# Half-array matmuls that take turns, in a decoder trunk on one core

## The chip, the core and the metric

The kernel runs on one core of a Trainium2 chip. TensorE multiplies: a stationary tile of up to 128 x 128 is loaded (a weight load, PEld in the profile), then a second operand streams through it. A product whose stationary tile has 64 columns or 64 rows uses half of the array. VectorE (DVE), ScalarE (ACT) and GpSimd (POOL) do the rest, SyncE (SP) issues the DMAs. The metric is the device time of one execution in microseconds, lower is better.

## What is computed

Two layers of a trunk over 1024 tokens of width 1024, all in f32. Each layer projects its input, runs three token mixers side by side, projects back, and ends with a gated convolutional feed-forward part. The parts of the reference that matter:

```python
# stick-breaking attention, 4 heads of 64, per block of 128 queries
z = einsum('bhqd,bhkd->bhqk', qb, k) * scale
log_keep = where(past, log_sigmoid(-z), 0.0)
log_later = cumsum(log_keep, axis=3, reverse=True) - log_keep
w = where(past, exp(log_sigmoid(z) + log_later), 0.0)
out = einsum('bhqk,bhkd->bhqd', w, v)

# softmax attention (MLA), 4 heads, queries and keys of 96, values of 64
p = softmax(where(causal, q @ k.T * scale, neg))
out = einsum('bhqk,bhkd->bhqd', p, v)

# RWKV-7, 8 heads of 64: a recurrence over tokens
sa = state @ -kk_t
state = state * w_t + outer(sa, kk_t * a_t) + outer(v_t, k_t)
y_t = state @ r_t
```

## The kernel before

Each layer goes through the same stages. First the projections with the first part of RWKV woven in (`phase_a`): `rw_stage1` handles two heads of 64 channels stacked on 128 partitions, in chunks of 64 tokens, and multiplies keys by queries within each chunk (L662). Head 0 lies in partitions 0 to 63, head 1 in 64 to 127, so each product has 64 rows: 4 products for head 0 into one PSUM bank, then 4 for head 1 into another. `rw_chain` then carries the state from chunk to chunk; its matmuls (L839, L847) write 64 partitions each, with 64 columns streaming. L839 goes to the two column halves in turns, L847 does one half of a chunk pair after the other.

Then attention. Four generators yield one block of 128 queries at a time: two softmax heads (`mla`, hp 0 and 1) and two stick-breaking heads (`stick`, hp 0 and 1). Each generator first goes through a head of pair 0 with key length growing from 128 to 1024, then through one of pair 1 with it shrinking from 1024 to 128; at the change of pair it loads and splits the new queries and keys. For stick-breaking pair 1 that split (L361, in four pieces each for q and k) is on GpSimd. `run` sorts the blocks of the four generators by step plus an offset, `STREAM_ORDER`, given in the order softmax 0, stick 0, softmax 1, stick 1.

A block makes its scores on TensorE (L202 to L204 with the mask product L539 for softmax, L376 and L377 for stick-breaking), weights on ScalarE, VectorE and GpSimd (L384 is the causal mask of stick-breaking, L385 to L388 the scan and product), transposes the weights 128 columns at a time (L327), copies them to one of six buffers `wt4` (L328) and multiplies by the values (`attn_out`, L312):

```python
for j in range(nb):
    self.nc.tensor.matmul(av, V[:, j, :], wt[:, j, :], start=j == 0, stop=j == nb - 1)
```

`V[:, j, :]` has 128 columns: the values of both heads of the pair. The result has 128 partitions, of which `av_store` copies the 64 of this head (L399) and stores them to DRAM. An f32 matmul appears as two records in the profile.

After attention, `oproj` multiplies the mixers' outputs by `w_o`, first split into high and low parts (`woh`, `wol`, `w0h`, `w0l`), and the feed-forward part follows.

What sets the order: every engine runs its instructions in a fixed order. A scheduler makes it when the kernel is built; it takes the program's order, the `PRIORITY` offsets of the helpers, and which buffers are free. A pool's buffers come free when the last reader is done.

Of the kernel before, what the change touches and what calls it, by code (L numbers as in the profile page):

```python
# [17 lines left out]
P = 128  # L18
# [12 lines left out]
C = 64  # L31
# [8 lines left out]
SPLIT_MLA = (0, 0)  # L40
SPLIT_STICK = (0, 4)
MLA_AHEAD = 4
STREAM_ORDER = (-3, 0, 0, 1)
Y_LAG = 2
PRIORITY = {
    "wload": 100,
# [23 lines left out]
class Body:  # L70
    def __init__(self, ctx, tc, a):
        self.ctx, self.tc, self.nc, self.a = ctx, tc, tc.nc, a
        self.n = 0
        self.ptags = {}
        self.rot = 0
        self.sq = 0
        self.sn = self.kn = 0

    def nm(self, s):
        self.n += 1  # L80
        return f"{s}_{self.n}"
# [20 lines left out]
    def ps1(self):  # L102
        return self.pst("ps")
# [203 lines left out]
            nc.vector.scalar_tensor_tensor(d[:, o + 1 : o + 512], ps[:, :511], mu, d[:, o + 1 : o + 512], op0=ALU.mult, op1=ALU.add)  # L307
        return d

    def attn_out(self, wt, nb, V, av):  # L310
        for j in range(nb):
            self.nc.tensor.matmul(av, V[:, j, :], wt[:, j, :], start=j == 0, stop=j == nb - 1)  # L312

    def pieces(self, LL):
        if LL <= 512:
# [65 lines left out]
    def stick_post(self, be, kp, i, LL, nb, n, V, hp, pr, wp):  # L381
        nc = self.nc
        dg = be[:, i * P : LL]
        nc.gpsimd.affine_select(out=dg, in_=dg, pattern=[[-1, P]], base=0, channel_multiplier=1, compare_op=ALU.is_gt, fill=-1.0)  # L384
        nc.vector.tensor_scalar(kp[:, : LL - 1], be[:, 1:LL], -0.5, 0.5, op0=ALU.mult, op1=ALU.add)  # L385
        kv = kp[:, : LL - 1][:, ::-1]
        nc.vector.tensor_tensor_scan(kv, kv, self.ones.to_broadcast([P, LL - 1]), 1.0, op0=ALU.mult, op1=ALU.mult)
        nc.vector.scalar_tensor_tensor(be[:, :LL], be[:, :LL], 1.0, kp[:, :LL], op0=ALU.add, op1=ALU.mult)  # L388
        wt = self.w_transpose(self.wt4[:, n % 6], be, nb, "pa")
        self.av_store(wt, nb, V, hp, self.mixd[pr], i, wp, "pa", 0.5)  # L390

    @prioritized
    def av_store(self, wt, nb, V, hp, dst, i, wp, tag, sc=1.0):
        nc = self.nc
        hr = slice(hp * 64, hp * 64 + 64)
        av = self.pst(tag)[:, :P]
        self.attn_out(wt, nb, V, av)
        ot = self.t(wp, [P, P], "avo", bufs=2)
        nc.scalar.mul(ot[hr], av[hr], sc)  # L399
        nc.sync.dma_start(dst[hr, i * P : i * P + P], ot[hr])  # L400

    def exact2(self, ps, st, src, tp, rows=slice(0, P)):
        hi, lo = (self.t(tp, [P, W2], n, F32R) for n in ("sh", "sl"))
# [145 lines left out]
    def mla_post(self, st, e, pcs, n, nb, sc, pr, hp, i, V, wp):  # L549
        nc = self.nc  # L550
        if n == 1:
            nc.vector.reciprocal(st[:, 6:7], st[:, 4:5])
        else:
            nc.scalar.activation(st[:, 7:8], st[:, 0:1], AF.Exp, scale=sc, bias=st[:, 3:4])
            nc.vector.scalar_tensor_tensor(st[:, 5:6], st[:, 4:5], st[:, 7:8], st[:, 5:6], op0=ALU.mult, op1=ALU.add)
            nc.vector.reciprocal(st[:, 6:7], st[:, 5:6])
        for u, (a0, a1) in enumerate(pcs):
            if u < n - 1:
                nc.vector.tensor_scalar(e[:, a0:a1], e[:, a0:a1], st[:, 7:8], st[:, 6:7], op0=ALU.mult, op1=ALU.mult)
            else:  # L560
                nc.vector.tensor_scalar(e[:, a0:a1], e[:, a0:a1], st[:, 6:7], None, op0=ALU.mult)
        self.sn += 1
        wt = self.w_transpose(self.wt4[:, self.sn % 6], e, nb)
        self.av_store(wt, nb, V, hp, self.mixd[2 + pr], i, wp, "av")

    def q2(self, tp):
        return self.t(tp, [P, W2], "q2", bufs=self.q2n)
# [33 lines left out]
    def rw_stage1(self, ft, hf, rkv, prep, Aa, tp):  # L601
        nc = self.nc
        tk = slice(hf * W2, hf * W2 + W2)
        pr_, pk, pvv = (t[:, tk] for t in rkv)
        L_, av, kk = (t[:, tk] for t in prep)
        ps1 = self.ps2
# [10 lines left out]
        AR = self.q4(tp).rearrange("p (a j e i) -> p a j e i", a=2, e=2, i=C)  # L617
        BK = self.q4(tp).rearrange("p (j e x i) -> p j e x i", e=2, x=2, i=C)
# [20 lines left out]
        flat = lambda t: t.rearrange("p a i -> p (a i)")  # L639
        for g in range(2):  # L640
            js = slice(2 * g, 2 * g + 2)
            RB = self.t(tp, [P, 2, 4, P], "RB", bufs=2)
            X = self.t(tp, [P, 2, 2, P], "X", bufs=2)
            pt = ps1()
            for q in range(2):
                j = 2 * g + q
                nc.tensor.transpose(pt[:, q * P : q * P + P], flat(AR[:, 0, j]), self.ident)
                nc.tensor.matmul(pt[:, (2 + q) * P : (3 + q) * P], pvv[:, j * P : j * P + P], self.cent, start=True, stop=True)
            pa = pt[:, 0:256].rearrange("p (q h k) -> p h q k", q=2, h=2)
            for h in range(2):  # L650
                nc.scalar.copy(X[:, h, :, h * C : h * C + C], pa[:, h])
            nc.scalar.copy(Vt[:, js, :], pt[:, 256:512].rearrange("p (q v) -> p q v", q=2))
            pb = ps1()
            for cc in range(4):
                nc.tensor.transpose(pb[:, cc * P : cc * P + P], flat(BK[:, 2 * g + cc // 2, cc % 2]), self.ident)
            pbv = pb.rearrange("p (c h k) -> p h c k", c=4, h=2)
            nc.scalar.copy(RB[:, :, :, C:P], pbv)
            for h in range(2):
                hr = slice(h * C, h * C + C)
                pA = ps1()  # L660
                for cc in range(4):
                    nc.tensor.matmul(pA[:, cc * P : cc * P + P], flat(BK[hr, 2 * g + cc // 2, cc % 2]), AR[hr, :, 2 * g + cc // 2, cc % 2, :], start=True, stop=True)  # L662
                pAv = pA.rearrange("p (c x) -> p c x", x=P)
                mk = self.maskA
                nc.vector.tensor_tensor(Aa[:, h, HC * hf + 4 * g : HC * hf + 4 * g + 4, :], pAv[:, :, 0:C], mk[:, None, 0:C].to_broadcast([P, 4, C]), op=ALU.mult)
                nc.vector.tensor_tensor(RB[:, h, :, 0:C], pAv[:, :, C:P], mk[:, None, C:P].to_broadcast([P, 4, C]), op=ALU.mult)
            pkv = ps1()[:, :256].rearrange("p (h q v) -> p h q v", h=2, q=2)
            for h in range(2):
                for q in range(2):
                    j = 2 * g + q  # L670
                    for e in range(2):
                        kr = slice(64 - 64 * e, 128 - 64 * e)
                        orow = slice(64 * e, 64 * e + 64)
                        nc.tensor.matmul(pkv[orow, h, q, :], Aa[kr, h, HC * hf + 2 * j + e, :], Vt[kr, j, h * C : h * C + C], start=True, stop=True)
            for h in range(2):
                nc.scalar.copy(X[:, h, :, C - h * C : P - h * C], pkv[:, h])
            gj = slice(4 * hf + 2 * g, 4 * hf + 2 * g + 2)
            RBv = RB.rearrange("p h (j e) x -> p h j (e x)", e=2)
            for h in range(2):
                nc.sync.dma_start(self.rbd[gj, :, 2 * ft + h].rearrange("j p x -> p j x"), RBv[:, h])  # L680
                nc.sync.dma_start(self.xxd[gj, :, 2 * ft + h].rearrange("j p x -> p j x"), X[:, h])
# [435 lines left out]
    def run(self):  # L1117
        nc, a, tc = self.nc, self.a, self.tc
# [27 lines left out]
        for l in range(L):  # L1146
# [7 lines left out]
            with ExitStack() as c:  # L1154
                self.psum(c, mm=(512, 3))
                self.psum(c, pi=(512, 1))
                cc = ExitStack()
# [4 lines left out]
            with ExitStack() as c:  # L1162
                self.psum(c, sc=(512, 2), av=(512, 2))
                aw = self.pool(c, "attn", bufs=2, side=side)
                ms = [self.mla(aw, hp) for hp in range(2)]
                self.wt4 = self.t(self.ip, [P, 6, NT, P], "Aa")
                self.kp3 = [self.t(self.ip, [P, S], n) for n in ("LA", "T", "pd")]
                for t in self.kp3:
                    nc.gpsimd.memset(t, 0.0)
                for _ in range(MLA_AHEAD):  # L1170
                    next(ms[0])
                cc.close()
                self.w0h = self.t(self.wq, [P, 2, D], "w0h", F32R)
                self.w0l = self.t(self.wq, [P, 2, D], "w0l", F32R)
                aw3 = self.pool(c, "attn3", bufs=2, side=other)
                st = [self.stick(aw3, self.ip, hp) for hp in range(2)]
                seq = sorted([(t + o, n, g) for n, (g, o) in enumerate(zip((ms[0], st[0], ms[1], st[1]), STREAM_ORDER)) for t in range(17)], key=lambda x: x[:2])
                for _, _, g in seq:
                    next(g, None)
                nxt = self.mix_load(NT - 1)  # L1180
                wr = [self.wo_load(l, k) for k in range(6)]
                for k in range(2):
                    self.split(self.w0h[:, k], self.w0l[:, k], wr[k], nc.gpsimd)
# [45 lines left out]
```

## Time and profile before

| | |
|---|---|
| runs before | 3151.69, 3152.36, 3153.42 us; median 3152.36 |
| profiled execution | 3154.05 us, span 3152.3 us |
| TensorE busy | 2993.2 us, 95% of the span, granted clock 0.981 on average |
| VectorE busy | 1796.4 us, 57% |
| ScalarE busy | 1058.6 us, 34% |
| GpSimd busy | 330.7 us, 10% |
| layer 0: attention | from 556.9 to about 746 us |
| layer 1: attention | from 2110.4 to about 2305 us |

Busy shares are means over stages with different limits; the rows further down give the stretches apart. A busy TensorE is not one at its peak: its matmuls overlap, and a record's length holds the time that its result needs to drain.

### The profile page before, as it was taken

The numbers are of one execution on the slowest core, as the hardware profiler recorded it, in microseconds if no ns is written. First come the engines' busy times: TensorE is split into PE (matmuls) and PEld (weight loads), VectorE is DVE, ScalarE is ACT, GpSimd is POOL, SyncE is SP. The second block draws the span as 40 slices with busy tenths as digits, with TensorE's granted clock in tenths as the row PEclk, the third lists the DMA queues.
The fourth block names the chain that finished last, engine by engine and source line by source line (L and its number), as shares of the span: only waits on it lengthen the run. The fifth ranks groups of instructions, "written<-read, shape, count | busy, mean of one in ns | idle before, by whom it ended". The sixth has DMA issues, their size and how long they took to land. (4 is left out here: it accounts for less than half of the span.)

```text
span 3152.3 us, 42021 instructions
## 1 busy us (share of the span) xinstructions
PE 2993.2 (95%) x16572; PEld 2421.2 (77%) x16572; DVE 1796.4 (57%) x2842; ACT 1058.6 (34%) x1865; POOL 330.7 (10%) x346
## 2 busy tenths in 40 slices
PE   8998999988999999999999989999789999999998
PEld 6677777776888888888877767777678888888887
DVE  4587764876644444444746877567865444344436
ACT  5444343764122112222144443446532211122220
POOL 0112131132000000000001111311310000000000
PEclk9999899999999999999999999999899999999999
DMA  4344566323421111111234456662235111111111
GB/s 129 97 141 110 169 186 191 97 62 121 149 85 50 51 41 47 54 50 51 64 84 127 108 132 193 178 190 53 81 121 172 54 47 40 43 56 49 54 47 54
DMA packets 339284, 301.79 MB, mean 96 GB/s; under 512 B 25224, under 2 KB 304016, under 8 KB 339088
## 3 DMA queue, kind: packets, MB, share of 16 engines
q1 hardware_dynamic: 339088, 299.11, 32.1%
q8 instruction: 131, 2.15, 0.3%
q14 instruction: 65, 0.53, 0.1%
HBM read 208.87 MB, written 90.18 MB: 95 GB/s over the span
## 5 line engine op out<-in xcount | busy, mean ns | idle before, releaser
L202 PE MATMUL psmm<-xTh,whi 128*128 128x512 f32 x2144 | 852.9, 398 | 0.0
L204 PE MATMUL psmm<-xTh,wlo 128*128 128x512 f32 x2144 | 852.1, 397 | 0.0
L203 PE MATMUL psmm<-xTl,whi 128*128 128x512 f32 x2144 | 852.1, 397 | 0.0
L197 ACT CAST whi<-raw 128x1024 fp32r<-128x1024 f32 x152 | 159.9, 1052 | 1111.3 <-PE psmm L203 1076.1
L204 PEld LDWEIGHTS psmm<-xTh,wlo 128*128 128x128 f32 x2144 | 405.2, 189 | 93.2 <-issue 4.3
L202 PEld LDWEIGHTS psmm<-xTh,whi 128*128 128x128 f32 x2144 | 405.4, 189 | 92.9 <-issue 4.4
L203 PEld LDWEIGHTS psmm<-xTl,whi 128*128 128x128 f32 x2144 | 405.3, 189 | 92.8 <-issue 3.9
L198 DVE TENSOR_TENSOR wlo<-raw,whi 128x1024 fp32r<-128x1024 f32 x122 | 148.8, 1220 | 424.5 <-ACT whi L197 424.5
L1031 DVE TENSOR_TENSOR y<-y,psps 128x512 f32<-128x512 f32 x288 | 196.2, 686 | 171.8 <-PE psps L204 171.4
L202 PE MATMUL psps<-wdh,hh 128*128 128x512 f32 x672 | 266.8, 397 | 0.0
L203 PE MATMUL psps<-wdl,hh 128*128 128x512 f32 x672 | 263.1, 391 | 0.0
L204 PE MATMUL psps<-wdh,hl 128*128 128x512 f32 x672 | 260.1, 391 | 0.0
L894 POOL TENSOR_TENSOR lrs<-lrs,mhalf 128x1 f32<-128x1 f32 x32 | 29.1, 910 | 1637.7 <-DVE lrs L893 1637.7
L202 PEld LDWEIGHTS psps<-wdh,hh 128*128 128x128 f32 x672 | 126.1, 188 | 36.4 <-ACT hh L197 5.5
L204 PEld LDWEIGHTS psps<-wdh,hl 128*128 128x128 f32 x672 | 126.2, 188 | 27.0
L203 PEld LDWEIGHTS psps<-wdl,hh 128*128 128x128 f32 x672 | 126.3, 188 | 25.8
L1006 DVE TENSOR_TENSOR cv<-cv,psmm 128x1024 f32<-128x1024 f32 x44 | 53.7, 1221 | 143.3 <-PE psmm L204 138.4
L198 DVE TENSOR_TENSOR wdl<-raw,wdh 128x1024 fp32r<-128x1024 f32 x42 | 51.4, 1225 | 88.5 <-ACT wdh L197 88.5
L198 POOL TENSOR_TENSOR wlo<-raw,whi 128x1024 fp32r<-128x1024 f32 x30 | 76.0, 2532 | 242.5 <-ACT whi L197 242.4
L312 PE MATMUL pspa<-Aa,mv 128*128 128x128 f32 x576 | 86.4, 298 | 4.4 <-ACT Aa L328 3.8
L312 PEld LDWEIGHTS pspa<-Aa,mv 128*128 128x128 f32 x576 | 77.1, 207 | 17.5 <-ACT Aa L328 15.8
L820 PE MATMUL pspa<-RBl,PSl 128*128 128x128 f32 x512 | 73.4, 292 | 17.2 <-ACT QC L823 11.8
(443 smaller groups left out, 4777.4 us busy)
## 6 DMA issues: line engine op xcount, KB each, us to landing
raw<-in_ffn_w_up_dram SPq DMA_DIRECT2D x88, 512.0 KB
raw<-in_w_in_dram SPq DMA_DIRECT2D x44, 512.0 KB
raw<-in_ffn_w_down_dram SPq DMA_DIRECT2D x44, 512.0 KB
rbd<-RB SPq DMA_DIRECT2D x64, 256.0 KB
PSl<-psd SPq DMA_DIRECT2D x32, 512.0 KB
RBl<-rbd SPq DMA_DIRECT2D x32, 512.0 KB
psd<-Vz SPq DMA_DIRECT2D x64, 128.0 KB
xxd<-X SPq DMA_DIRECT2D x64, 128.0 KB
```

Source lines behind the costliest of these rows:

```text
L197: self.nc.scalar.copy(hi, src)
L198: (eng or self.nc.vector).tensor_tensor(lo, src, hi.bitcast(F32), op=ALU.subtract)
L202: mm(out, lh, rh, start=start, stop=False)
L203: mm(out, lh, rl, start=False, stop=False)
L204: mm(out, ll, rh, start=False, stop=stop)
L312: self.nc.tensor.matmul(av, V[:, j, :], wt[:, j, :], start=j == 0, stop=j == nb - 1)
L820: nc.tensor.matmul(pQ[:, f, e, :], PSh[:, f, h, e, :], RBh[:, f, h, e, :], start=True, stop=True)
L894: nc.gpsimd.tensor_tensor(rs, rs, self.mhalf[:, 0:1], op=ALU.pow)
L1006: nc.vector.tensor_tensor(cv, cv, pg, op=ALU.mult)
L1031: nc.vector.tensor_tensor(y[:, i, hs], y[:, i, hs], ps, op=ALU.add)
```

## The change

Four edits. `attn_out` takes the weights of both heads of a pair and multiplies each by its own 64 value columns, into its own 64 partitions of one PSUM tile, head 0 and head 1 in turns. For that, `pair` holds the first head's weights until the second's are there; then one copy and one store carry both. In `rw_stage1` the 8 key-query products of a group go to the two row halves in turns, with both PSUM banks taken at the start. `in_order` adds dependencies that keep these turns on TensorE. And the generators' offsets become (-2, 0, -2, 0), with the four softmax blocks that run ahead shared by the two heads.

```diff
-STREAM_ORDER = (-3, 0, 0, 1)
+STREAM_ORDER = (-2, 0, -2, 0)
...
+    def in_order(self, ms):
+        for a, b in zip(ms, ms[1:]):
+            self.tc.add_manual_dep(b.ins, a.ins.name, mybir.DependencyInfo(mybir.DependencyClass.NoSync, mybir.DependencyReason.DATA), reason="array halves take turns")
+
-    def attn_out(self, wt, nb, V, av):
+    def attn_out(self, wts, nb, V, av):
+        ms = []
         for j in range(nb):
-            self.nc.tensor.matmul(av, V[:, j, :], wt[:, j, :], start=j == 0, stop=j == nb - 1)
+            for hp in range(2):
+                hc = slice(hp * 64, hp * 64 + 64)
+                ms.append(self.nc.tensor.matmul(av[hc], V[:, j, hc], wts[hp][:, j, :], start=j == 0, stop=j == nb - 1))
+        self.in_order(ms)
...
-        self.av_store(wt, nb, V, hp, self.mixd[pr], i, wp, "pa", 0.5)
+        self.pair(("s", pr, i), wt, hp, nb, V, self.mixd[pr], i, wp, "pa", 0.5)
+
+    def pair(self, key, wt, hp, *args):
+        if key in self.pairs:
+            wts = [wt, wt]
+            wts[1 - hp] = self.pairs.pop(key)
+            self.av_store(wts, *args)
+        else:
+            self.pairs[key] = wt
...
-        nc.scalar.mul(ot[hr], av[hr], sc)
-        nc.sync.dma_start(dst[hr, i * P : i * P + P], ot[hr])
+        nc.scalar.mul(ot, av, sc)
+        nc.sync.dma_start(dst[:, i * P : i * P + P], ot)
...
+            pAs = [ps1(), ps1()]
+            ms = []
+            for cc in range(4):
+                for h in range(2):
+                    hr = slice(h * C, h * C + C)
+                    ms.append(nc.tensor.matmul(pAs[h][:, cc * P : cc * P + P], flat(BK[hr, 2 * g + cc // 2, cc % 2]), AR[hr, :, 2 * g + cc // 2, cc % 2, :], start=True, stop=True))
+            self.in_order(ms)
             for h in range(2):
-                hr = slice(h * C, h * C + C)
-                pA = ps1()
-                for cc in range(4):
-                    nc.tensor.matmul(pA[:, cc * P : cc * P + P], flat(BK[hr, 2 * g + cc // 2, cc % 2]), AR[hr, :, 2 * g + cc // 2, cc % 2, :], start=True, stop=True)
-                pAv = pA.rearrange("p (c x) -> p c x", x=P)
+                pAv = pAs[h].rearrange("p (c x) -> p c x", x=P)
...
-                for _ in range(MLA_AHEAD):
-                    next(ms[0])
+                for t in range(MLA_AHEAD):
+                    next(ms[t % 2])
```

In the changed file the lines are 9 to 19 further down: L320 is the value product (before L312), L336 the transposes (L327), L370 the split on GpSimd (L361), L393 the mask (L384), L385 and L386 the stick-breaking scores (L376, L377). In the rows that follow a size is that of the result, and "x4" counts matmuls that stand unbroken.

TensorE, first half of attention in layer 0. Before, with softmax value products (psav) and stick-breaking ones (pspa) beside transposes of weights (mexp):

```order
L312 MATMUL psav_5400<-Aa_4944,mv_4951 128x128 x2
L312 MATMUL pspa_5433<-Aa_4944,mv_5237 128x128
L327 MATMUL psav_5460<-ident_60,mexp_5439 128x128 x4
L327 MATMUL psav_5466<-ident_60,mexp_5439 128x128 x3
L327 MATMUL pspa_5493<-ident_60,mexp_5482 128x128
L377 MATMUL pspq_5530<-kl_945_5414,qh_943_5412 128x256
L327 MATMUL pspa_5493<-ident_60,mexp_5482 128x128 x2
L202 MATMUL pssc_5552<-kh_920_5311,qh_918_5309 128x512
L312 MATMUL psav_5471<-Aa_4944,mv_5303 128x128 x7
L312 MATMUL pspa_5498<-Aa_4944,mv_5237 128x128 x3
```

The same stretch in the changed program:

```order
L320 MATMUL psav_5491<-Aa_4944,mv_4951 64x128 x14
L203 MATMUL pssc_5595<-kh_841_4986,qh_839_4984 128x512
L204 MATMUL pssc_5595<-kl_842_4987,qh_839_4984 128x512
L205 MATMUL pssc_5595<-kh_841_4986,ql_840_4985 128x512
L555 MATMUL pssc_5595<-negm_67,identr_65 128x128
L320 MATMUL pspa_5657<-Aa_4944,mv_5184 64x128
L203 MATMUL pssc_5685<-kh_986_5677,qh_984_5675 128x512
L336 MATMUL psav_5557<-ident_60,mexp_5536 128x128 x4
L336 MATMUL psav_5563<-ident_60,mexp_5536 128x128 x4
L320 MATMUL pspa_5657<-Aa_4944,mv_5184 64x128 x7
```

Two heads' products now stand in one run; in some pairs the first product stands alone, with scores and transposes between it and the rest.

GpSimd, layer 0, where the stick-breaking heads change to pair 1: qh and kl are the new queries and keys, a mexp is one block's mask. Before:

```order
L361 TENSOR_TENSOR kl_1122_6254<-pst_6247,kh_1121_6253 128x256 x3
L384 AFFINE_SELECT mexp_6102<-mexp_6102 128x128
L361 TENSOR_TENSOR kl_1122_6254<-pst_6247,kh_1121_6253 128x256
L361 TENSOR_TENSOR qh_1120_6252<-pst_6246,qh_1120_6252 64x256 x4
L384 AFFINE_SELECT mexp_6187<-mexp_6187 128x128
L384 AFFINE_SELECT mexp_6265<-mexp_6265 128x128
L384 AFFINE_SELECT mexp_6362<-mexp_6362 128x128
L361 TENSOR_TENSOR qh_1168_6488<-pst_6482,qh_1168_6488 64x256 x4
L384 AFFINE_SELECT mexp_6401<-mexp_6401 128x128
L361 TENSOR_TENSOR kl_1170_6490<-pst_6483,kh_1169_6489 128x256 x4
```

In the changed program:

```order
L393 AFFINE_SELECT mexp_6176<-mexp_6176 128x128
L370 TENSOR_TENSOR qh_1105_6321<-pst_6315,qh_1105_6321 64x256 x4
L393 AFFINE_SELECT mexp_6248<-mexp_6248 128x128
L370 TENSOR_TENSOR kl_1107_6323<-pst_6316,kh_1106_6322 128x256 x4
L370 TENSOR_TENSOR qh_1121_6397<-pst_6391,qh_1121_6397 64x256 x4
L370 TENSOR_TENSOR kl_1123_6399<-pst_6392,kh_1122_6398 128x256 x4
L393 AFFINE_SELECT mexp_6334<-mexp_6334 128x128
```

The sets of the two heads, which had three masks between them, now stand together with one mask among them; the first mask of the new pair (mexp_6334) comes after all four groups.

TensorE, end of attention in layer 0. The output projection (psmm, of the high and low parts w0h, w0l, woh, wol) before:

```order
L202 MATMUL psmm_7133<-w0h_5060,whi_7064 128x512
L203 MATMUL psmm_7133<-w0l_5061,whi_7064 128x512
L312 MATMUL pspa_7058<-Aa_4944,mv_6244 128x128
L204 MATMUL psmm_7133<-w0h_5060,wlo_7065 128x512
L202 MATMUL psmm_7133<-woh_7101,whi_7064 128x512
L203 MATMUL psmm_7133<-wol_7102,whi_7064 128x512
```

In the changed program, a little ahead of the last value products:

```order
L320 MATMUL pspa_6761<-Aa_4944,mv_6313 64x128 x10
L336 MATMUL pspa_6786<-ident_60,mexp_6775 128x128 x4
L385 MATMUL pspq_6864<-kh_1106_6322,qh_1105_6321 128x256
L386 MATMUL pspq_6864<-kl_1107_6323,qh_1105_6321 128x256
L203 MATMUL psmm_7005<-woh_6973,whi_6936 128x512
L204 MATMUL psmm_7005<-wol_6974,whi_6936 128x512
L336 MATMUL pspa_6803<-ident_60,mexp_6792 128x128 x4
L320 MATMUL pspa_6809<-Aa_4944,mv_6313 64x128
L205 MATMUL psmm_7005<-woh_6973,wlo_6937 128x512
```

The first products with woh and wol, which came after the last value product, now stand among the last stick-breaking blocks.

## Rows read from the trace of the kernel before

**Rows 1.** Busy time by stretches: length, each engine's busy us (instructions), clock, DMA, GB/s.

```profile
100.00:545.00 445.00, 411.37 (x3071) 326.39 (x3070) 300.37 (x551) 185.47 (x349) 96.33 (x91) 0.96 0.52 152
556.90:650.00 93.10, 86.06 (x609) 73.76 (x608) 76.16 (x181) 68.64 (x195) 11.11 (x23) 1.00 0.28 76
650.00:746.00 96.00, 80.94 (x532) 69.65 (x530) 74.64 (x119) 56.58 (x146) 32.04 (x32) 0.91 0.26 71
746.00:758.00 12.00, 6.59 (x20) 3.98 (x20) 8.96 (x6) 5.92 (x7) 5.22 (x2) 0.86 0.70 213
```

**Rows 2.** Groups by line, 556.9 to 746: count, busy us, mean ns, idle before.

```profile
L312 PE MATMUL pspa<-Aa,mv 128*128 128x128 f32 x288 | 43.9, 301 | 1.9 <-ACT Aa L328 1.7
L312 PE MATMUL psav<-Aa,mv 128*128 128x128 f32 x288 | 39.8, 283 | 1.4 <-ACT Aa L328 0.5
...
L399 ACT ACTIVATE avo<-pspa 64x128 f32<-64x128 f32 x32 | 8.7, 271 | 15.6 <-PE pspa L312 6.7 <-issue 4.0 <-ACT mexp L378 3.0
...
L399 ACT ACTIVATE avo<-psav 64x128 f32<-64x128 f32 x32 | 8.7, 270 | 11.1 <-PE psav L312 5.2 <-ACT Aa L328 1.9 <-ACT mst L554 1.5
```

**Rows 3.** Timeline of TensorE at two value runs: start us, length us, then the instruction.

```profile
596.74 1.50 PE L312 MATMUL psav<-Aa,mv 128*128 128x128 f32 x12
598.08 0.83 PE L312 MATMUL pspa<-Aa,mv 128*128 128x128 f32 x6
```

**Rows 4.** Timeline of TensorE at state products; first, record lengths min/median/max.

```profile
L839 PE MATMUL pspq<-S,QC x256: 222/222/368, 396.9 to 2106.5; 128*64 128x64 f32 x128
...
426.27 0.40 PE L204 MATMUL psmm<-xTh,wlo 128*128 128x512 f32 x1
426.60 0.45 PE L839 MATMUL pspq<-S,QC 128*64 128x64 f32 x8
426.98 0.50 PE L202 MATMUL psmm<-xTh,whi 128*128 128x512 f32 x1
427.31 0.39 PE L203 MATMUL psmm<-xTl,whi 128*128 128x512 f32 x1
427.55 0.39 PE L204 MATMUL psmm<-xTh,wlo 128*128 128x512 f32 x1
...
517.44 0.68 PE L847 MATMUL pspy<-S,QC 128*64 128x64 f32 x8
```

**Rows 5.** Timeline of TensorE at key-query products: one head alone, then two.

```profile
166.84 1.16 PE L662 MATMUL pspa<-q,q 64*128 64x128 f32 x8
...
169.87 0.82 PE L662 MATMUL pspa<-q,q 64*128 64x128 f32 x5
170.42 0.37 PE L662 MATMUL pspy<-q,q 64*128 64x128 f32 x1
...
170.85 0.72 PE L662 MATMUL pspy<-q,q 64*128 64x128 f32 x5
```

**Rows 6.** Timeline of TensorE behind layer 0's attention; in brackets idle time and its end.

```profile
745.35 0.49 PE L312 MATMUL pspa<-Aa,mv 128*128 128x128 f32 x2
...
747.26 0.50 PE L202 MATMUL psmm<-woh,whi 128*128 128x512 f32 x1 [1.20 <-ACT woh L197]
749.72 0.79 PE L203 MATMUL psmm<-wol,whi 128*128 128x512 f32 x1 [1.95 <-POOL wol L198]
...
754.12 0.50 PE L203 MATMUL psmm<-wol,whi 128*128 128x512 f32 x1 [1.48 <-DVE wol L198]
```

**Rows 7.** Timeline of GpSimd at layer 0's change of pair.

```profile
649.82 7.13 POOL L361 TENSOR_TENSOR qh<-pst,qh 64x256 fp32r<-64x256 f32 x4
...
674.88 5.77 POOL L361 TENSOR_TENSOR qh<-pst,qh 64x256 fp32r<-64x256 f32 x4 [0.95 <-ACT qh L350]
...
680.98 5.72 POOL L361 TENSOR_TENSOR kl<-pst,kh 128x256 fp32r<-128x256 f32 x4
```

**Rows 8.** Timeline of TensorE at the change of pair, layer 0 and layer 1.

```profile
654.78 1.94 PE L327 MATMUL pspa<-ident,mexp 128*128 128x128 f32 x8 [3.12 <-DVE mexp L388]
...
2241.58 0.80 PE L376 MATMUL pspq<-kh,qh 128*128 128x512 f32 x1 [7.46 <-POOL qh L361]
```

More of the change, by code (lines that the diff above doesn't have):

```diff
@@ L77, in __init__ @@
         self.sn = self.kn = 0
+        self.pairs = {}
     def nm(self, s):
@@ L389, in stick_post, with av_store @@
         wt = self.w_transpose(self.wt4[:, n % 6], be, nb, "pa")
-        self.av_store(wt, nb, V, hp, self.mixd[pr], i, wp, "pa", 0.5)
+        self.pair(("s", pr, i), wt, hp, nb, V, self.mixd[pr], i, wp, "pa", 0.5)
[6 more added lines that the diff above has]
+            self.pairs[key] = wt
     @prioritized
-    def av_store(self, wt, nb, V, hp, dst, i, wp, tag, sc=1.0):
+    def av_store(self, wts, nb, V, dst, i, wp, tag, sc):
         nc = self.nc
-        hr = slice(hp * 64, hp * 64 + 64)
         av = self.pst(tag)[:, :P]
-        self.attn_out(wt, nb, V, av)
+        self.attn_out(wts, nb, V, av)
         ot = self.t(wp, [P, P], "avo", bufs=2)
-        nc.scalar.mul(ot[hr], av[hr], sc)
-        nc.sync.dma_start(dst[hr, i * P : i * P + P], ot[hr])
+        nc.scalar.mul(ot, av, sc)
+        nc.sync.dma_start(dst[:, i * P : i * P + P], ot)
     def exact2(self, ps, st, src, tp, rows=slice(0, P)):
@@ L563, in mla_post @@
         wt = self.w_transpose(self.wt4[:, self.sn % 6], e, nb)
-        self.av_store(wt, nb, V, hp, self.mixd[2 + pr], i, wp, "av")
+        self.pair(("m", pr, i), wt, hp, nb, V, self.mixd[2 + pr], i, wp, "av", 1.0)
     def q2(self, tp):
```

## The prediction

> **What bounds the kernel now.** I read the busy table by stretches first [rows 1]. In the first half of a layer's attention (557 to 650 us) TensorE is busy 86.06 of 93.1 us and VectorE 76.16: TensorE sets the pace, VectorE is close behind. In the second half (650 to 746) they are busy 80.94 and 74.64 of 96: both wait for each other and for ScalarE and GpSimd. Just after it, 746 to 758, TensorE does 6.59 us of work in 12. Before attention, from 100 to 545, it is busy 411.37 of 445. These stretches come twice, once per layer, and everything after them is dense matmul that the change does not touch.
>
> Next, the groups by line within one layer's attention [rows 2]: the value products (L312) are 576 records, two for each f32 matmul, and are the largest thing on TensorE there. The timeline tells what one costs [rows 3]: 12 records start at 596.74 and the next run at 598.08, so 0.112 us a record, 576 x 0.112 = 64.5 us a layer. Half of each result is thrown away: a 128-column stationary tile holds two heads, and one is kept.
>
> **Do halves of the array overlap here?** The state update (L839) already alternates between column halves, with 64 columns streaming [rows 4]: 8 records take 0.45 us, while 8 records of L847 in one half take 0.68. Take off one record's length, 0.222 at the median, and the seven steps are 0.033 apart when alternating, 0.066 in one half. The two halves do run at once. For row halves with 128 columns streaming, the key-query products show it [rows 5]: 8 records in one half take 1.16 us, but with the other half queued behind them, 16 end at 170.85 + 0.72 = 171.57, that is 1.70 us after 169.87, with pspa and pspy records lying over one another in the middle.
>
> The Trainium skill says otherwise for columns ("TensorE: Matmul & The Clock Gate", Part 3): weight loads overlap running matmuls only where the row group differs, and two column halves share their row groups. By that the value products would gain nothing. The trace disagrees where 64 columns stream [rows 4]; no row shows it for 128. It is the first rival below.
>
> **What the split costs.** Entering and leaving a half-array run is not free [rows 4]. L204 at 426.27 is followed by L839 at 426.60 (0.33, where two wide matmuls stand 0.24 apart, 427.31 to 427.55), and L202 at 426.98 by L203 at 427.31 (0.33 again). From 426.27 to 427.31 is 1.04; two wide steps are 0.48 of it, so the run cost 0.56, of which 8 x 0.033 = 0.26 is its own work: 0.30 us per run.
>
> **Value products.** The change issues the same 576 records a layer, each 64 columns wide in the stationary tile, in pairs. If a pair takes 0.112 as one record did, that is 32.3 us. In the order of the changed program the 576 matmuls of both layers stand in 107 unbroken runs, because the scheduler puts other matmuls in between; 47 of them are one matmul alone, with no partner. Odd runs leave a half idle: 4 us a layer. 53 runs x 0.30 = 16 us a layer. So 64.5 becomes 52: 12.5 us of TensorE a layer. Bounds: 28 if switching were free and all runs were even (32.3 saved less 4), and less than nothing if halves do not overlap (the first rival). I take 12.5, which rests on a run of the nearest form.
>
> How much of it ends the layer earlier? In the first half TensorE idles only 7 us of 93, so of 6.25 I count 5.5. In the second half, where it idles 15 of 96, I count 2.5 of 6.25. The value work of ScalarE halves too: 64 result copies of 0.27 us [rows 2] become 32, 8.7 us a layer on an engine with slack (68.64 of 93.1 busy), so at nothing; its cover is that slack. 64 stores fewer in all on SP: nothing, no chain waits for them but the last. **8 us a layer.**
>
> **The new stream order** has two effects. First, both softmax heads now run two blocks ahead, so their buffers come free before the last stick-breaking blocks, and the output weights can be split into high and low parts during attention's end. Before, those splits come after the last value product at 745.35, and TensorE stands 1.20, 1.95 and 1.48 us for them [rows 6], 4.6 in all. In the changed order 24 output-projection matmuls stand ahead of the last value product, against 5 before. But they stand in TensorE's queue between small blocks, so a late split (a ScalarE cast, a GpSimd subtraction) can now hold a block behind it. **4 us a layer**, bounds 0 to 4.6.
>
> Second, both stick-breaking heads change pair together. GpSimd then subtracts for both back to back. One head's set took 7.13 us or 5.77 us (q) and 5.72 us (k) [rows 7]; two sets are some 23 us with one block's mask in between. The first masks of the new pair are queued behind all four groups, VectorE's scans behind the masks, and TensorE's transposes behind those. Before, the two heads came some 28 us apart and TensorE stood still 3.12 us in layer 0 and 7.46 in layer 1 at these places [rows 8]. What covers it now on TensorE, by the changed order: 26 pairs of value products (5.8 us at 0.224), 33 transposes (3.7 at 0.112), some 18 score matmuls at 0.24 or less, and the switches: about 15 us. I reckon 23 less 15, so 8 us once, against 3.12 plus a few smaller gaps and 7.46: **1 us a layer lost**; bounds -3 to +10.
>
> **Key-query products.** Before, a group of 16 records takes 1.70 us in one piece, or 2 x 1.16 in two [rows 5]. Alternating, 8 steps of 0.112 plus the last record's 0.27 make 1.17. The order has 64 unbroken runs where there were 48, since the first product of a group often stands alone, so I take 0.3 to 0.4 us per group instead of 0.5: 16 groups a layer, 5 us of TensorE. There TensorE is busy 92% of the stretch and otherwise waits, so **2.5 us a layer**. The masks of head 0 now wait for the PSUM bank of head 1 as well; bound: 0.5 us x 16 = 8 lost, or 5 gained.
>
> **Sum.** 8 + 4 - 1 + 2.5 = 13.5 us a layer, 27 in all. The profiled execution took 3154.05 us (span 3152.3), so 3127; the median of the runs is 1.7 lower, so 3125.
>
> **Rivals.**
> 1. Column halves do not overlap with 128 columns streaming. Then the value products stay at 64.5 + 16 = 80 us a layer, 16 more. Against it: the alternating L839 run. For it: it streams 64 columns only. With 12 of the 16 visible, + 12 - 4 + 1 - 2.5 = 6.5 a layer: 3165. Chance 0.06.
> 2. GpSimd's double set decides. If the work behind the masks cannot start and TensorE covers only 5 of the 23 us, it stands 18, which is 13 more a layer than before; the other terms are 14.5. It decides from about 20 us of standing on: slower from there. At the worst all 23 us are bare, 18 more than before, and some 4 us go to the slower clock behind the gap (the second half was granted 0.91 on average, a mix of 1.2 and 2.4 GHz, the first half 1.00 [rows 1]): 22 lost against 14.5 gained, 15 in all: 3167. Chance 0.06.
> 3. The change does what it says but is hidden: VectorE ends the stretches (76.16 of 93.1 and 74.64 of 96 busy), and only a quarter of TensorE's gain and the tail show: 3 + 4 - 1 = 6 a layer, 3140. Chance 0.23, some of it within 0.2%.
> 4. All of it shows, and switching costs nothing beside neighbours that stream 128 columns: 20 + 4.6 + 5 = 29 a layer: 3094. Chance 0.12.
>
> **How the numbers follow.** The forecast has 0.53. Its own bounds are about 3110 to 3140. The range takes in rival 3 whole and most of rival 4: 3098 to 3148, leaving out rivals 1 and 2 and the ends. A measurement of this kernel tells 0.2%, 6.3 us, from no change: faster means below 3146. Forecast and rival 4 are faster, and most of rival 3 (0.15 of 0.23): 0.80. Within 0.2%: 0.11, from rival 3 and the mild part of 2. Slower: 0.09.
>
> **What would show it.** Value products at 0.056 us a record within runs of 10 or more: halves overlap; 0.112 and rival 1 holds. A wide matmul 0.33 after its neighbour at each run's end: the switch price. Attention shorter by 8 us in its first two thirds, and no TensorE gap over 1 us on the output weights: the terms of 8 and 4. A single TensorE gap of some 8 us at the pair change, ended by VectorE's or GpSimd's work on the new pair; if it is 20, rival 2. Key-query groups of 1.2 us. The prediction is wrong if attention keeps its length although TensorE's busy time there falls (rival 3), or if the stretch from 100 to 545 grows because the masks come later.

## The result and the profile after

The changed kernel took 3114.07 us at the median, against 3152.89 for the kernel before; the ratio is 0.9875, with a 95% interval from 0.9858 to 0.9893. That is 39.4 us gained (34 to 45), where 27 were forecast. All effects below are given as ratios to the kernel before, timed on the same chip; 0.001 is 3.15 us.

Where the time went is read from four stretches: each layer's projections and recurrent part up to its last product, and attention with the output projection behind it. The view is busy time by stretches, with the columns of [rows 1]; first the kernel before, then the changed one.

```profile
129.90:561.90 432.00, 394.57 (x3062) 314.34 (x3062) 295.36 (x568) 184.36 (x358) 95.71 (x92) 0.96 0.53 154
561.90:849.10 287.20, 261.08 (x1549) 218.13 (x1548) 213.34 (x384) 143.09 (x357) 52.34 (x60) 0.96 0.32 95
1690.20:2115.40 425.20, 384.79 (x3064) 309.80 (x3063) 296.69 (x568) 185.09 (x360) 92.71 (x92) 0.96 0.55 157
2115.40:2407.90 292.50, 258.56 (x1547) 217.63 (x1546) 214.09 (x384) 142.82 (x355) 53.95 (x61) 0.96 0.31 93
```

```profile
129.00:560.60 431.60, 389.80 (x3061) 301.61 (x3060) 298.00 (x572) 185.86 (x360) 92.49 (x91) 0.96 0.52 154
560.60:834.70 274.10, 245.56 (x1553) 188.96 (x1552) 209.56 (x380) 134.19 (x323) 55.20 (x61) 0.95 0.32 100
1675.10:2104.30 429.20, 387.40 (x3064) 303.82 (x3063) 296.44 (x571) 185.72 (x360) 92.73 (x92) 0.95 0.55 155
2104.30:2370.50 266.20, 239.68 (x1550) 185.60 (x1550) 209.52 (x380) 133.76 (x322) 52.00 (x61) 0.97 0.34 102
```

Attention with the output projection became shorter by 13.1 us in layer 0 and by 26.3 in layer 1. The stretches ahead of it, where the key-query products are, became 0.4 shorter and 4.0 longer: nothing came of that part of the change. (Four kernels of the experiments, e4, e9, e10 and f4, give TensorE the same order of work there; their stretches take 430.7 to 436.1 us and 422.7 to 428.3. So a few us are the scatter of single executions.)

**Value products.** The timeline of TensorE in the changed kernel, to be set beside [rows 3]:

```profile
616.31 1.97 PE L320 MATMUL psav<-Aa,mv 128*64 128x128 f32 x32
618.21 0.50 PE L205 MATMUL pssc<-kh,ql 96*128 96x512 f32 x1
```

Thirty-two records stand between 616.31 and 618.21, 0.059 each with the run's end in it; the step inside such a run is 0.055, half of the 0.112 of before. Column halves run at once with 128 columns streaming too. Summed over each layer without idle time (each value record up to the start of the next instruction), the value products took 71.4 and 69.6 us before, and 48.3 and 46.5 after: 23 us a layer less.

**Pair change and tail.** The GpSimd sets of both heads in layer 0, then the gaps of TensorE at that time and at the pair change of layer 1, then TensorE's gaps on the output projection, and VectorE at the last of them; they answer to [rows 6 to 8].

```profile
649.59 3.91 POOL L370 TENSOR_TENSOR qh<-pst,qh 64x256 fp32r<-64x256 f32 x4 [2.22 <-ACT qh L359]
653.58 0.62 POOL L393 TENSOR_SCALAR_AFFINE_SELECT mexp<-mexp 128x128 f32<-128x128 f32 x1
656.11 6.75 POOL L370 TENSOR_TENSOR kl<-pst,kh 128x256 fp32r<-128x256 f32 x4 [1.91 <-ACT kh L360]
662.94 3.78 POOL L370 TENSOR_TENSOR qh<-pst,qh 64x256 fp32r<-64x256 f32 x4
666.80 2.91 POOL L370 TENSOR_TENSOR kl<-pst,kh 128x256 fp32r<-128x256 f32 x4
```

```profile
651.41 0.96 PE L336 MATMUL pspa<-ident,mexp 128*128 128x128 f32 x7 [2.35 <-DVE mst L561]
662.34 0.55 PE L336 MATMUL psav<-ident,mexp 128*128 128x128 f32 x3 [2.67 <-DVE mexp L575]
...
2192.14 1.68 PE L336 MATMUL pspa<-ident,mexp 128*128 128x128 f32 x7 [2.35 <-DVE mst L561]
2203.05 1.21 PE L336 MATMUL psav<-ident,mexp 128*128 128x128 f32 x4 [2.71 <-DVE mexp L575]
```

```profile
718.01 0.50 PE L204 MATMUL psmm<-wol,whi 128*128 128x512 f32 x1 [1.85 <-POOL wol L199]
...
738.10 0.50 PE L203 MATMUL psmm<-w0h,whi 128*128 128x512 f32 x1 [1.30 <-ACT whi L198]
...
747.29 0.50 PE L203 MATMUL psmm<-w0h,whi 128*128 128x512 f32 x1 [2.54 <-DVE z L964]
```

```profile
746.54 0.69 DVE L964 SCALAR_TENSOR_TENSOR z<-z,psmm 128x512 f32<-128x512 f32 x1 [7.24 <-DMA z<-in_x_dram]
```

The double set takes 20 us, from 649.59 to 669.71. TensorE has two gaps in that time, 2.35 and 2.67, both ended by VectorE's softmax work and neither by the set directly; layer 1 has the same two, and its gap of 7.46 on the set [rows 8] is gone. The tail keeps its gaps: 5.7 us in three, against 4.6 in three in [rows 6]. But the last of them is a new one. VectorE adds the layer's input, `z`, to the projected result and stands 7.24 us idle for the load of `z`: SyncE issues that load at 740.30, just after the last store of attention has landed at 740.10. In the kernel before, TensorE was still waiting for splits while that load came.

**Key-query products.** TensorE at one group of the changed kernel, beside [rows 5]:

```profile
147.16 0.48 PE L679 MATMUL pspa<-q,q 64*128 64x128 f32 x2
...
152.22 0.37 PE L679 MATMUL pspy<-q,q 64*128 64x128 f32 x1
152.23 0.37 PE L679 MATMUL pspa<-q,q 64*128 64x128 f32 x1
152.44 0.27 PE L679 MATMUL pspy<-q,q 64*128 64x128 f32 x1
152.44 0.27 PE L679 MATMUL pspa<-q,q 64*128 64x128 f32 x1
...
153.00 0.38 PE L679 MATMUL pspy<-q,q 64*128 64x128 f32 x2
```

The first product runs alone at 147.16; its partner, in the bank taken second, comes 5 us later, and since the order is fixed the other six wait behind that one. From there the halves alternate at 0.11 a pair, as forecast. Over the 32 groups, the first mask on VectorE starts 4.33 us after a group's first product at the mean; before it was 2.14.

### The profile page after: what moved, and what is told of

Read it like the earlier page. It is cut to its first block, busy times and chain, and to the rows that moved or that the text cites. A ratio compares the mean times of both kernels' runs of the same rounds, so it can differ in the third digit from the quotient of the medians.

```text
span 3114.1 us, 41891 instructions
## 1 busy us (share of the span) xinstructions
PE 2955.1 (95%) x16572; PEld 2339.9 (75%) x16572; DVE 1790.4 (57%) x2842; ACT 1043.3 (34%) x1801; POOL 328.5 (11%) x346
## 5 line engine op out<-in xcount | busy, mean ns | idle before, releaser
L1020 ACT ACTIVATE cv<-cv 128x1024 f32<-128x1024 f32 x44 | 46.7, 1061 | 115.8 <-DVE cv L1019 115.8
L839 PEld LDWEIGHTS pspa<-RBl,PSl 128*128 128x128 f32 x512 | 64.9, 197 | 25.2 <-ACT QC L842 11.2
```

The lines of the kernel that those rows point to most:

```text
L839: nc.tensor.matmul(pQ[:, f, e, :], PSh[:, f, h, e, :], RBh[:, f, h, e, :], start=True, stop=True)
L1020: nc.scalar.activation(cv, cv, AF.Gelu)
```

## Experiments

**Which part of the change pays in attention?** Two theories: the gain is TensorE time, since the column halves overlap; or it is the new stream order, which brings the weight splits forward. Four kernels take the change apart.

*e1_order_only*: the kernel before, with this alone:

```
-STREAM_ORDER = (-3, 0, 0, 1)
+STREAM_ORDER = (-2, 0, -2, 0)
...
-for _ in range(MLA_AHEAD): next(ms[0])
+for t in range(MLA_AHEAD): next(ms[t % 2])
```

> The kernel before with the new stream order and the new head start alone; value products stay one head at a time at 128 columns, key-query products as before. Theory (the gain is TensorE time: two column halves at once): from attention's start to the last output-projection matmul, TensorE's busy time fell by 34 us over both layers between the two traces and its idle time by only 5, so the order alone is worth about 5, at most 12: 3141 to 3150. Rival (the gain is the order: weight splits earlier, the 7.46 us stall of layer 1 gone): most of the 39 us stay, 3115 to 3128.

Measured: 1.0014 (1.0004 to 1.0023), 4 us slower. Both theories missed it; the rival is refuted outright for the order alone. Its tail stands longer than before, as the timeline of TensorE shows, and a gap of the pair change is there too; the last line is VectorE:

```profile
677.97 0.80 PE L376 MATMUL pspq<-kh,qh 128*128 128x512 f32 x1 [5.71 <-POOL qh L361]
...
738.04 0.80 PE L203 MATMUL psmm<-wol,whi 128*128 128x512 f32 x1 [4.24 <-DVE wol L198]
...
760.43 0.80 PE L202 MATMUL psmm<-w0h,whi 128*128 128x512 f32 x1 [4.25 <-DVE z L945]
...
759.69 0.69 DVE L945 SCALAR_TENSOR_TENSOR z<-z,psmm 128x512 f32<-128x512 f32 x1 [10.02 <-DMA z<-in_x_dram]
```

The output matmuls that stand early in the queue wait at 738.04 for a split on a VectorE that is still at attention's work. At 760.43 they wait for the load of `z`, which comes only behind the last store of attention. (Pairs with the old order were not tried: a head's weights wait in one of six tiles for their partner, and the softmax heads would be three blocks apart. So what the order is worth beside the pairs was not measured.)

*e4_same_half*: the changed kernel without the alternation.

```
-        for j in range(nb):
-            for hp in range(2):
+        for hp in range(2):
+            for j in range(nb):
```

> The changed kernel, but the value products of a block go head by head: all of head 0's in the left column half, then all of head 1's in the right, in a fixed order. Pairing, stores, stream order and the 64-column weights stay; only the alternation goes. Theory: records of one half step at 0.11 us instead of 0.055, so TensorE gets 32 us more a layer less some fewer switches (92 runs for 107); nearly all of it shows, as the saving did: 3155 to 3175. Rival (the gain is the order, or the halved copies): 3110 to 3125.

Measured: 0.9928 (0.9915 to 0.9942), 16.7 us slower than the changed kernel, and 22.7 faster than before. Neither forecast. TensorE at a run of 32:

```profile
621.73 3.33 PE L320 MATMUL psav<-Aa,mv 128*64 128x128 f32 x32
624.99 0.51 PE L205 MATMUL pssc<-kh,ql 96*128 96x512 f32 x1
```

3.26 us, against 1.90 with the alternation (a little under 32 x 0.11, since the two heads overlap where one ends). So the alternation is real, and half-width products one after the other step nearly as slowly as those of full width. But pairing without overlap is worth at least about as much as the alternation (22.7 against 16.7 us, the second known to about 7).

*e10_pair_full_width* and *e9_two_copies* divide the pairing. The first issues both heads when the second is ready, but at full width, each with its PSUM tile, copy and store. The second is the changed kernel with two copies and two stores:

```
(e10)  for hp in range(2):
           av = self.pst(tag)[:, :P]
           for j in range(nb): matmul(av, V[:, j, :], wts[hp][:, j, :], ...)
           copy and store rows hr of av
(e9)   -nc.scalar.mul(ot, av, sc); dma_start(dst[:, ...], ot)
       +for hr in (slice(0, 64), slice(64, 128)):
       +    nc.scalar.mul(ot[hr], av[hr], sc); dma_start(dst[hr, ...], ot[hr])
```

> The changed kernel with each head's value products at full width of 128 columns, one head after the other, each with its own PSUM tile, copy and store, but both issued only when the second head of the pair is ready. So only the time of issue is that of the changed kernel. Rival of the above (the time of issue makes the gain): 3128 to 3138, as in the kernel without alternation. Theory (copies and PSUM tiles make it): 3148 to 3160, as with the stream order alone.

> The changed kernel with two result copies and two stores per pair, half the rows each, as before; the alternation stays. Theory (the pairing's gain without alternation, some 26 us, is the halved copies and the earlier free PSUM bank): 64 copies at 0.27 us are 17 us of ScalarE, and 3121 to 3132. Rival (ScalarE has slack, the gain lies in when the products are issued): 3112 to 3119.

Measured: e10 0.9980 (0.9971 to 0.9989), in the range of the theory of copies and PSUM tiles; e9 0.9927 (0.9914 to 0.9940), a little past the upper end of its theory (the halved copies) and far from the rival's. The four corners add up:

| | two copies and stores | one copy and store |
|---|---|---|
| no overlap | e10 0.9980 | e4 0.9928 |
| alternating | e9 0.9927 | changed 0.9875 |

Alternation is worth 0.0053 in either column, and one copy and store instead of two 0.0052 in either row, some 16.5 us each; each of these steps is known to 5 to 7 us. The two steps into the changed kernel change one thing each. The two out of e10 hold more, since e10 also has full-width products and two PSUM tiles. Every kernel also got an order of its own from the scheduler: in the attention of e4 and e9, 290 to 500 of some 1550 matmul records stand elsewhere than in the changed kernel. Attention and output projection of the four, first both layers of e10, then e4, e9 (the changed kernel's rows stand above):

```profile
563.00:847.10 284.10, 257.75 (x1553) 217.90 (x1553) 215.49 (x381) 142.09 (x353) 57.46 (x61) 0.97 0.32 96
2113.40:2398.10 284.70, 257.54 (x1547) 218.04 (x1547) 210.52 (x379) 142.14 (x352) 60.21 (x60) 0.96 0.32 95
```

```profile
563.30:841.80 278.50, 257.61 (x1552) 206.32 (x1552) 210.70 (x380) 133.57 (x323) 56.77 (x61) 0.97 0.32 98
2111.50:2390.20 278.70, 256.83 (x1550) 206.95 (x1550) 212.06 (x380) 134.80 (x322) 52.84 (x61) 0.97 0.31 98
```

```profile
558.20:834.70 276.50, 244.61 (x1552) 188.27 (x1552) 212.35 (x380) 143.36 (x354) 57.28 (x61) 0.95 0.33 99
2104.80:2380.30 275.50, 238.80 (x1549) 184.18 (x1548) 211.10 (x379) 143.49 (x353) 55.01 (x61) 0.96 0.33 99
```

Length less TensorE's busy time is its idle time. From e10 to e4, fewer copies, busy time stays and idle falls from 26.4 and 27.2 to 20.9 and 21.9. From e10 to e9, alternation, busy falls by 13.1 and 18.7, and idle grows to 31.9 and 36.7: about half of what TensorE is spared turns into waiting, which ends for the most part on VectorE (20 us of it in layer 0 of e9). The two gains come by different ways, which fits that they add.

*f4_one_copy_two_stores*: one copy for both halves, `dma_start` twice.

> The changed kernel with one result copy per pair, but two stores, half the rows each. Theory (of the 18.8 us between one copy with one store and two with two, the copies on ScalarE make nearly all): 3113 to 3119. Rival (the stores and SyncE's queue make it): 3125 to 3134.

Measured: 0.9909 (0.9895 to 0.9923): 10.7 us for the second store alone, and 5.7 more for the second copy. That is the lower end of the rival's range, but each step is known only to 6 or 7 us, so the copy's part can't be told from nothing. How a store on SyncE costs that much stays open: in its profile, layer 0's attention is as long as the changed kernel's (273.8 against 274.1) and layer 1's is 8 longer (274.2 against 266.2), where the scheduler also laid out the work in another order (430 of 1548 matmul records stand elsewhere). The stretches ahead, which the edit leaves alone, differ by 4.5 and -6.5. A part may be the order and not the store.

**The key-query products.** Theory: as made, the edit costs a little. Rival: it gains the 5 us predicted.

*e2_kq_only* is the kernel before with the key-query edit; *e3_av_no_kq* is the changed kernel with the old key-query lines:

```
 pAs = [ps1(), ps1()]
 for cc in range(4):
     for h in range(2):
         ms.append(matmul(pAs[h][...], ...))
 self.in_order(ms)
```

> The kernel before with the key-query products alternating between the row halves in a fixed order, both PSUM banks taken first; nothing else. Theory: this edit costs time, since the two stretches it lies in came out 3.6 us longer in all in the changed kernel: 3153 to 3160, and a TensorE gap of some 4 us at the second set of groups (near 195 us). Rival: it gains the predicted 5 us, and what the changed kernel lost there came from elsewhere: 3146 to 3150.

> The changed kernel with the key-query products of before (head by head, no fixed order). Theory: 3.6 us better than the changed kernel, 3107 to 3112. Rival (the key-query edit gains 5): 3117 to 3121.

Measured: e2 1.0011 (1.0002 to 1.0020), e3 0.9880 (0.9866 to 0.9893), which can't be told from the changed kernel. The first theory's forecast for e2 held, and e3 came out between the two. Alone the edit costs some 3 us; beside the rest it neither gains nor costs what can be measured. Yet the products themselves take less of TensorE: summed as above, 33.3 and 31.4 us in the two layers before, and 23.8 in each after. In e2 they take as little, but TensorE's busy time in the two stretches falls only from 779.4 to 775.6 us. The projections' matmuls woven in between take 16 us more: at the full clock 218 of them, where it was 143, stand beside a product on half of the array, and there one takes 0.12 us longer than among its like; that is 9 of the 16. TensorE's idle time grows by 4 us as well. The reason for both would be the lone first product, which opens the group early, puts other matmuls into its middle and leaves the masks waiting. If so, the cure is to begin with the partner that becomes ready last. The same holds for the value pairs, where 47 of 107 runs are a lone product of the earlier head.

*e5_late_first* does it for the value pairs, *e6_late_first_both* for the key-query groups as well:

```
-            for hp in range(2):             # value pairs
+            for hp in (late, 1 - late):
...
-                for h in range(2):          # key-query groups, e6 only
+                for h in (1, 0):
```

> The changed kernel, but each value pair begins with the head whose weights come last, so the first product can no longer run ahead alone: in the order the value runs fall from 107 to 74, single products from 47 to 7. Theory (a lone product costs a switch and an idle half): 33 runs fewer at about 0.2 us, and 40 idle halves at 0.11, 11 us of TensorE in all, of which some 40% shows, as between the kernels with and without alternation (43 us of TensorE gave 16.6): 3107 to 3112. Rival (the lone products filled time in which TensorE waited anyway, and now the pair starts later): 3113 to 3120.

> The same, and in the key-query groups the row half whose PSUM bank is taken second goes first: key-query runs fall from 64 to 40, single products from 26 to 2. Theory: 24 switches fewer, 5 us of TensorE, and the group no longer waits in its middle: 2 to 4 below the kernel with late-first value pairs alone, 3103 to 3110. Rival (the groups' masks, not TensorE, set the pace): no difference from it, within 2 us.

Measured: e5 0.9848 (0.9835 to 0.9861), 8.5 us below the changed kernel, and e6 0.9772 (0.9759 to 0.9785), 24 us below e5. At 3083.47 us e6 beats both kernels, the one before by 72 us and the changed one by 32. The forecast for e5 held; that for e6 was far too small. TensorE at the same group of e6, then the stretch ahead of attention in both layers of e5 and of e6:

```profile
153.98 0.35 PE L679 MATMUL pspy<-q,q 64*128 64x128 f32 x1
153.99 0.37 PE L679 MATMUL pspa<-q,q 64*128 64x128 f32 x1
...
154.84 0.27 PE L679 MATMUL pspy<-q,q 64*128 64x128 f32 x1
154.87 0.27 PE L679 MATMUL pspa<-q,q 64*128 64x128 f32 x1
```

```profile
129.60:561.00 431.40, 392.48 (x3061) 303.77 (x3061) 294.64 (x570) 185.63 (x360) 96.86 (x92) 0.96 0.52 154
1665.60:2094.50 428.90, 387.38 (x3063) 303.52 (x3063) 295.14 (x572) 185.48 (x360) 94.21 (x92) 0.95 0.55 156
```

```profile
130.80:549.60 418.80, 378.64 (x3062) 297.86 (x3061) 294.10 (x570) 185.30 (x360) 93.95 (x92) 0.97 0.54 159
1657.00:2071.40 414.40, 374.48 (x3064) 297.08 (x3063) 293.20 (x572) 185.22 (x360) 93.81 (x92) 0.97 0.56 162
```

The group runs in one piece, and the stretches are 12.6 and 14.5 us shorter, nearly all of it TensorE's busy time (13.8 and 12.9). The key-query products account for 4.4 and 5.3 of that; the transposes before them and the small products behind them, which also stand in fewer pieces, for about half of the rest. The clock has a share in all of it: of the two stretches e5 spent 75 us at the lower of its two levels (0.5 of the full clock), e6 55, and there a wide matmul stands 0.43 us from the next in place of 0.23, so an estimated 9 us. The mean time from first product to first mask is back to 2.06 us.

*f1_kq_late_only* puts the late-first key-query edit alone on the kernel before. *f2_kq_grouped* takes e5 and issues the key-query products head by head, unbroken, the late bank first:

```
(f1)  e2 with   for h in (1, 0):
(f2)  e5 with   for h in (1, 0):
                    for cc in range(4):
```

> The kernel before with the key-query products alternating, the row half whose PSUM bank is taken second first; nothing else (value products and stream order as before). Theory (the edit itself is worth some 24 us, and a lone first product per group hid it): 3128 to 3135. Rival (it pays only beside the changed attention, which shares its scheduler): 3140 to 3156.

> The kernel with late-first value pairs (3107), but the key-query products of a group go head by head in a fixed order, the head of the second PSUM bank first: 36 unbroken runs, hardly any alternation of row halves. Theory (what pays is the unbroken group, with the few switches that go with it): within 5 us of the kernel with both late first, 3083 to 3090. Rival (what pays is the overlap of the row halves): 3095 to 3110.

Measured: f1 0.9918 (0.9904 to 0.9932): the edit alone, in the right order, is worth 26 us, and in the order that the change has it loses 3. The time, 3127.57, lies just below the theory's range; the rival (that it pays only beside the changed attention) fell. In f1 TensorE's busy time in the two stretches is 745.8 us, against 779.4 before, and its idle time is the same. f2 0.9839 (0.9823 to 0.9855): unbroken groups without overlap give 3 us of the 24 that e6 gained, no more than the noise, so here the rival was right. The products took 26.7 and 29.0 us in f2's layers, 19.1 and 18.6 in e6's. Thus both are needed: the alternation of the row halves pays 21 us, but only in a group that starts when both its banks are free. The clock is not taken apart from it: f2's executions were granted 0.974 to 0.979 on average, those of e6 0.979 to 0.982.

*f6_copies_on_vector*: e6 with the result copy on VectorE.

```
-        nc.scalar.mul(ot, av, sc)
+        nc.vector.tensor_scalar(ot, av, sc, None, op0=ALU.mult)
```

> The kernel with both late first (3083), with the one result copy per pair on VectorE instead of ScalarE. Theory (VectorE, busy 87% of the stretch, is the nearer limit, and a copy that waits there for a value product holds the scans behind it): 3086 to 3100. Rival (ScalarE's queue, held behind copies that wait for value products, is the limit): 3070 to 3081.

Measured: 0.9798 (0.9782 to 0.9813), 8 us slower than e6, as the theory had it. Layer 1's attention up to its last value product, e6 and then f6:

```profile
2071.40:2244.00 172.60, 145.87 (x1131) 112.44 (x1129) 150.57 (x285) 116.34 (x298) 48.57 (x54) 0.92 0.29 83
```

```profile
2067.70:2245.20 177.50, 145.76 (x1131) 111.79 (x1129) 156.16 (x315) 110.74 (x268) 48.76 (x54) 0.92 0.28 82
```

VectorE has 5.6 us more to do and the stretch is 4.9 longer, though ScalarE has 5.6 less; in layer 0 the stretch is 1.5 longer. Behind the freed TensorE, VectorE is a nearer limit than ScalarE. Whether its busy time or the wait of a copy in its queue does it was not taken apart.

## Why the prediction was right, and where it was not

The direction and the range held: 3114 lies between 3098 and 3148. The point, 3125, was 11 us too slow, and the sum came that near by errors that partly cancelled, which was luck.

- **Value products: the visible part right, its two factors wrong.** The sum said 25 us of TensorE freed over both layers, of which 16 show. Measured: 46 less (71.4 + 69.6 less 48.3 + 46.5), and the alternation shows 16.5. The time after, 52 a layer, was near (47.4); the time before was not 64.5 but 70.5, since 576 x 0.112 left out that the first record of a run takes 0.19 before too, and that records at the lower clock take 0.21. The share that shows was taken as 0.64 from TensorE's idle time; it was a third to a half (from e4 to the changed kernel the products' sum falls by 37 us, from e10 to e9 by 52, and 16.5 show in either).
- **Copies and stores: the step that failed most.** They were costed at nothing, with ScalarE's slack as cover. Halving them was worth 16.5 us. The warning stood in [rows 2]: before the copies ScalarE idles 15.6 and 11.1 us, much of it on the value product itself. ScalarE is in the middle of the chain and takes its instructions in order, so a copy that waits can hold what stands behind it; that this is what cost the time was not tested. After, the same groups of a layer read:

```profile
L415 ACT ACTIVATE avo<-pspa 128x128 f32<-128x128 f32 x16 | 4.5, 281 | 9.2 <-PE pspa L320 8.2 <-ACT woh L198 0.7
L415 ACT ACTIVATE avo<-psav 128x128 f32<-128x128 f32 x16 | 4.5, 279 | 9.9 <-PE psav L320 9.4 <-ACT mexp L562 0.3
```

  Half the copies, and 19.1 us of waiting for 26.7. How the 16.5 divides between copy and store is not settled (f4).
- **Stream order: wrong sign.** It was to bring 4 - 1 = 3 us a layer, 6 in all; alone it loses 4; beside the pairs it was not measured. The 24 early output matmuls are there, but what they wait for is late. In e1 that is a split (4.24), as in the warning that a late split can hold a block behind it. And it is the load of `z` (2.54 in the changed kernel, 4.25 in e1), a wait that the prediction does not have: the splits after attention used to cover it. That the pair change would cost no more than a few us was right in the changed kernel, where it even saves layer 1 its gap of 7.46, and not in e1 (5.71).
- **Key-query products: 5 us predicted, none came.** The group was to take 1.17 us. The products saved more than that assumed (33.3 to 23.8 in layer 0), but the lone first product, counted as a mere switch of its own run, is where the gain went: it let the group wait in its middle, and the wide matmuls beside the pieces took 16 of the 17 us back. The bound named for it, 0.5 us on the masks of head 0, should have been 2.2 (4.33 less 2.14).
- **Issue at the pair** was not a term. From e1 to e10 the ratio falls by 0.0034, 10.7 us, with the key-query edit in it. Why was not tested.
- **Rivals.** The first is refuted by 0.055 a record. By the Trainium skill ("TensorE: Matmul & The Clock Gate", Part 3) a weight load overlaps running matmuls only where the row group differs; the column halves here share theirs and still take 0.055 a record in turns against 0.112, so the measurement decides. The second is refuted by gaps of 2.35 and 2.67 where 18 were feared. The third was half right: much of TensorE's gain is hidden behind VectorE, as f6 and the idle time of e9 say; what made up for it was the part of the copies and stores, which the rival did not have either. The fourth did not happen.

## What to carry to other kernels

When two products are tied to take turns, begin with the one whose operands or bank come last; tied the other way round, the first runs off alone and the pair waits in its middle (24 us here for exchanging two loop values). Sum the neighbours too: what a product saves can go to the matmuls beside it. Freed time on one engine is worth what the next engine leaves of it, and the small copies behind it are not free because their engine has slack: look at what that engine waits for ahead of them, and who stands behind. Take a change with several parts apart on a square of four kernels; here two gains of some 16.5 us added up within the noise, and one of them was a part costed at nothing.

## What the runs showed of the hardware

- Column halves of TensorE overlap in full with 128 columns streaming: 0.055 us a record alternating, against 0.112 for full width; 32 records in 1.90 us against 3.26 in one half after the other.
- Going out of half-array products into transposes costs about 0.09 us: a transpose (L336) starts 0.203 us after the last value record at the median, and 0.112 in the kernel before, where the value products have full width. Beside wide matmuls it is 0.12 at each end: in the changed kernel's stretches ahead of attention, at the full clock, 218 wide matmuls stand beside a half-array product, and they take 25 us more in all than as many among their like.
- A GpSimd subtraction can hold VectorE for its whole length. In the changed kernel, first GpSimd and VectorE, then TensorE behind them; last the same VectorE operation in the kernel before, twice in 0.76:

```profile
192.75 2.37 POOL L199 TENSOR_TENSOR wlo<-raw,whi 128x1024 fp32r<-128x1024 f32 x1 [4.13 <-ACT whi L198]
192.84 2.56 DVE L648 TENSOR_TENSOR q<-ta,q 128x256 f32<-128x256 f32 x1
195.46 1.11 PE L671 MATMUL pspq<-ident,q 128*128 128x128 f32 x4 [4.29 <-DVE q L648]
```

```profile
189.01 0.76 DVE L632 TENSOR_TENSOR q<-ta,q 128x256 f32<-128x256 f32 x2
```

  0.38 us of work took 2.56 beside the 2.37 of GpSimd, and TensorE, which needs the result, stood 4.29 in all. The Trainium skill ("SBUF — State Buffer", section "SBUF: two separate sides") has VectorE operations with two SBUF inputs and GpSimd operations share a pair of ports, which the one that starts first holds for its whole instruction; the trace agrees here (GpSimd starts 0.09 earlier, VectorE ends 0.28 later).
